# A streaming encoder layer on one core: stick-breaking products partly on GpSimd, the causal mask as a TensorE matmul, and another spread of the filler work

## The chip, the cores and the metric

One core of a Trainium2 chip runs the whole program. The metric is device time in microseconds, from one launch. The engines are called by the names of the profile: PE (TensorE matmuls), PEld (its weight loads), DVE (VectorE), ACT (ScalarE), POOL (GpSimd) and SP, whose queue issues the DMAs.

## The reference

One layer for 1024 prompt tokens and 64 sample tokens (the sample also sees 1024 cached keys), all in f32. Two groups of heads work side by side: four heads of differential attention and eight of stick-breaking attention.

```
h = rmsnorm(x) * (1 + scale1) + shift1;  u = h @ w_in         # q, k, v of both groups
z = (q . k) / 8                                               # stick-breaking heads
log_keep = where(k_pos < q_pos, log_sigmoid(-z), 0)
between  = reverse_cumsum(log_keep) - log_keep                # over the keys behind this one
w        = where(k_pos < q_pos, exp(log_sigmoid(z) + between), 0)
osb      = w @ v
x = x + gate1 * rmsnorm(concat(od, osb) @ w_out)
x = x + gate2 * rmsnorm(relu(h2 @ w_up)^2 @ w_down)
```

In words: the weight of a key is sigmoid(z) of its own, times the product of sigmoid(-z) over all keys between it and the query. Keys at or behind the query's own place count as nothing: their sigmoid(z) must be 0 and their sigmoid(-z) must be 1.

## The kernel before

**Exactness.** f32 operands are cut into a rounded part and a rest (`split`, L62 to L65: ACT makes the rounded copy `hi`, DVE, or GpSimd where `el` says so, subtracts it to get `lo`), and a product is two or three matmuls that add up in PSUM.

**Stages.** First come the modulation vectors and the first projections, then eight units of attention, u = 0 to 3 for the differential heads and u = 4 to 7 for the stick-breaking heads (two heads each), then the output projection (`py`) and the feed-forward network (`pu`, `pd`) for 870 us.

**A unit** is a list of steps. For u of 4 and more a step is `Stick(u, q, hd)`: query blocks t = 2q and 2q + 1 (128 rows each) of head hd. For each t and each chunk of up to 512 keys, `qk` (L571) makes the scores `pz` with two matmuls, ACT takes `s` = sigmoid(z) and `k` = sigmoid(-z) (L738, L739). Then `earlier` (L717) puts 0 into `s` and 1 into `k` on and above the diagonal of the last 128 columns, with two selects on GpSimd. Then `stick` (L705) goes over the chunks from the last one (c = n - 1) to the first: DVE runs a product scan over `k` from right to left (L712), carries it on from the chunk behind, and multiplies `s` by the scanned `k` (L713); one column between two chunks is done on GpSimd (L715). There are 12 chunks for each unit and head, 96 in all, with 1 chunk for t up to 3 and 2 chunks above. Later `apply` (L745) transposes `s` by PE (`pt`, L586), splits the result into `ah` and `al`, multiplies by the values (`po`, L759 and L760) and writes the output columns `mx` (L778, L779).

`Sample(u)`, one in each unit, does the 64 sample tokens against the cache, with scores `pzS`, and for u of 4 and more calls `stick` as well, with three chunks of 512, 512 and 64.

**Order.** Steps overlap: `apply` of one step is merged with `score` of the next (L1013). Each yields its cost, and `Filler.spend` emits that much of other work in between: the projections of the units to come (`proj`, matmuls at L303 to L305, three groups g for each unit) and 12 pieces of modulation rows (`rows`, matmuls at L201 that wait for 1 MB of weights by DMA). The ratio of filler to step cost is set so that the next marked projection is done in time (L1010), from the steps' `cost`. The filler list puts 2, 2, 2, 2, 1 and 3 pieces of `rows` behind the last projection of units 2 to 7 (L994). A scheduler then sets each engine's order.

**V.** `proj_v` (L519) transposes the projected values by PE into a PSUM bank (`pnv`), copies them to `ov` for the output, and splits the bank into the two halves of `V`, the rest on DVE (L542, by L65).

**Buffers.** Tiles `s` and `k` come from one tag "s" with 11 buffers of 128 x 512; the scores use two PSUM banks of the tag "qk". All GpSimd work stands in one queue: selects, the column products, the query pads `qz` (L442), the rests of weight splits (128 x 1024, `wq`, `wk`, `wv`, `wo`) and of the cached values `cv`.

## Time and profile before

| | |
|---|---|
| Time, median of 3 runs | 1587.48 us (1587.13 to 1589.22) |
| Profiled execution, its own time | 1589.58 us |
| Its span, first to last instruction | 1587.9 us |
| PE busy | 1517.0 us (96%), 8682 matmuls |
| DVE busy | 987.2 us (62%) |
| ACT busy | 703.3 us (44%) |
| POOL busy | 366.7 us (23%) |
| Mean granted TensorE clock | 0.973 of 2.4 GHz |

Busy time of an engine is the time in which one of its instructions was open, a wait inside the instruction included. Matmuls overlap each other, so a duration of a PE row is longer than the distance to the next one.

### The profile page before, as it was taken

The page shows a single profiled execution, that of the slowest core. Times are in us where ns is not written, and L with a number is a line of the kernel's source. Part 1 is how long each engine was busy: PE and PEld are TensorE (multiplying, and loading weights), DVE is VectorE, ACT ScalarE, POOL GpSimd, SP SyncE. Part 2 cuts the span into 40 slices and gives each one's busy share as a digit, 9 for nine tenths or more (in the row PEclk, how much of TensorE's full clock was granted, in tenths as well). Part 3 has the DMA queues.
Part 4 walks back from the last instruction along what each step waited for, and adds up shares of the span by engine and source line. Part 5 has one row for each costly group of instructions (what it writes and reads, how often), then busy time and mean ns, then how long its engine had stood idle before and what let it go on. Part 6 is the DMA issues. An engine that isn't in the chain of part 4 may idle for free.

```text
span 1587.9 us, 23684 instructions
## 1 busy us (share of the span) xinstructions
PE 1517.0 (96%) x8682; PEld 1357.9 (86%) x8682; DVE 987.2 (62%) x1880; ACT 703.3 (44%) x1665; POOL 366.7 (23%) x580
## 2 busy tenths in 40 slices
PE   6899999999999999789999999999999999999998
PEld 3689988988888889667889888999999899999896
DVE  3777676778789888995552455445544445544447
ACT  3867675766666667656563221121221121221132
POOL 0444352526353434451120000000000000000003
PEclk9999999998999999879999999999999999999999
DMA  9322142432322222364220222021111011111025
GB/s 309 115 60 87 55 116 84 135 95 76 95 74 85 69 70 78 103 208 161 97 63 27 80 80 78 17 79 53 54 42 52 28 41 53 54 41 53 27 80 179
DMA packets 152518, 133.22 MB, mean 84 GB/s; under 512 B 11233, under 2 KB 136274, under 8 KB 152402
## 3 DMA queue, kind: packets, MB, share of 16 engines
q1 hardware_dynamic: 152402, 131.71, 27.2%
q8 instruction: 68, 1.11, 0.3%
q14 instruction: 48, 0.39, 0.1%
HBM read 108.59 MB, written 23.09 MB: 83 GB/s over the span
## 4 chain that ended last, share of the span: by engine, by line
PE 74%; DVE 12%; issue 4%; ACT 3%; DMA 2%; POOL 1%; SPq 0%; POOLq 0%; DVEq 0%; ACTq 0%
PE pu L303 8%; PE pu L304 8%; PE pu L305 8%; PE pd L1145 8%; PE pd L1146 8%; PE pd L1148 7%; DVE k L712 4%; PE py L1059 2%; PE py L1060 2%; PE pt L586 2%; DVE s L713 2%; PE py L1062 2%; PE pq L304 1%; PE pq L303 1%; PE pq L305 1%
## 5 line engine op out<-in xcount | busy, mean ns | idle before, releaser
L1152 DVE TENSOR_TENSOR acc<-pd,acc 128x512 f32<-128x512 f32 x252 | 171.9, 687 | 113.3 <-PE pd L1148 107.2
L1130 ACT ACTIVATE sq<-pu 128x384 f32<-128x384 f32 (+1 forms) x96 | 45.2, 471 | 310.8 <-PE pu L305 310.8
L1131 DVE TENSOR_TENSOR sq<-sq 128x384 f32<-128x384 f32 (+1 forms) x96 | 72.1, 751 | 174.7 <-ACT sq L1130 174.7
L65 DVE TENSOR_TENSOR al<-pt,ah 128x512 fp32r<-128x512 f32 (+2 forms) x128 | 75.5, 599 | 25.7 <-ACT ah L64 24.9
L575 PE MATMUL pz<-K,Q 128*128 128x512 f32 (+2 forms) x192 | 74.8, 393 | 6.4 <-ACT k L739 2.2
L64 ACT CAST ah<-pt 128x512 fp32r<-128x512 f32 (+2 forms) x128 | 65.4, 523 | 33.6 <-PE pt L586 23.2
L586 PE MATMUL pt<-ident,s 128*128 128x128 f32 x432 | 73.7, 288 | 3.3 <-DVE s L713 2.6
L624 ACT ACTIVATE s<-s,mn 128x512 f32<-128x512 f32 (+3 forms) x96 | 58.5, 611 | 26.7 <-DVE mn L660 25.4
L576 PE MATMUL pz<-Kl,qz 128*128 128x512 f32 (+2 forms) x192 | 69.8, 369 | 0.0
L712 DVE TENSOR_TENSOR_SCAN k<-k 128x127 f32<-128x127 f32 (+3 forms) x64 | 62.1, 980 | 4.3 <-POOL k L720 4.0
L713 DVE TENSOR_TENSOR s<-s,k 128x383 f32<-128x383 f32 (+3 forms) x96 | 62.9, 662 | 1.4
L586 PEld LDWEIGHTS pt<-ident,s 128*128 128x128 f32 x432 | 53.1, 147 | 7.6 <-DVE s L713 3.3
L65 DVE TENSOR_TENSOR rl<-sq,rh 128x384 fp32r<-128x384 f32 x64 | 35.7, 558 | 37.9 <-ACT rh L64 37.9
L738 ACT ACTIVATE s<-pz 128x512 f32<-128x512 f32 (+2 forms) x96 | 48.1, 501 | 16.5 <-PE pz L576 12.0
L575 PEld LDWEIGHTS pz<-K,Q 128*128 128x128 f32 x192 | 38.3, 200 | 15.1 <-ACT k L739 4.5
L64 ACT CAST rh<-sq 128x384 fp32r<-128x384 f32 x64 | 32.9, 514 | 40.2 <-DVE sq L1131 38.2
L739 ACT ACTIVATE k<-pz 128x512 f32<-128x512 f32 (+2 forms) x96 | 48.4, 504 | 4.9 <-DVE k L712 4.0
L442 POOL CAST qz<-Q 64x256 fp32r<-64x256 f32 x64 | 34.7, 542 | 66.3 <-PE pz L576 63.9
L760 PE MATMUL po<-al,V 128*128 128x256 f32 (+1 forms) x160 | 43.5, 306 | 6.7 <-DVE al L65 6.6
L759 PE MATMUL po<-ah,V 128*128 128x256 f32 (+1 forms) x160 | 44.9, 292 | 0.5 <-ACT ah L64 0.5
L720 POOL TENSOR_SCALAR_AFFINE_SELECT s<-s 128x128 f32<-128x128 f32 x64 | 30.1, 470 | 63.6 <-ACT s L738 62.9
L660 DVE CUSTOM_DVE_ANT_0 s<-pz,T 128x512 f32<-128x512 f32 (+3 forms) x64 | 37.2, 585 | 10.8 <-PE pz L576 10.3
(1227 smaller groups left out, 5211.3 us busy)
## 6 DMA issues: line engine op xcount, KB each, us to landing
arr<-in_w_ada SPq DMA_DIRECT2D x16, 512.0 KB
arm<-in_w_ada SPq DMA_DIRECT2D x16, 512.0 KB
ar<-in_w_ada SPq DMA_DIRECT2D x10, 512.0 KB
mixD<-mx SPq DMA_DIRECT2D x32, 128.0 KB
xr<-in_x_prompt SPq DMA_DIRECT2D x16, 256.0 KB
xD<-xr SPq DMA_DIRECT2D x16, 256.0 KB
xy<-xD SPq DMA_DIRECT2D x8, 512.0 KB
out_y_prompt<-xy SPq DMA_DIRECT2D x16, 256.0 KB
```

What stands on the lines that cost most here:

```text
L64: (eh or nc.scalar.copy)(hi, src)
L65: (el or nc.vector).tensor_tensor(lo, src, fr(hi), ALU.subtract)
L303: mm(ps[:, :n], lhsT=wh[:, k, :], rhs=hh[:, k, :n], start=(k == 0), stop=False)
L304: mm(ps[:, :n], lhsT=wh[:, k, :], rhs=hl[:, k, :n], start=False, stop=False)
L305: mm(ps[:, :n], lhsT=wl[:, k, :], rhs=hh[:, k, :n], start=False, stop=(k == 7))
L575: mm(ps[:, :w], lhsT=S["Q"][m][:, qt], rhs=S["Kd"][m][:, c0 : c0 + w], start=True, stop=False)
L586: nc.tensor.transpose(pt[:kr, i * P : (i + 1) * P], a, ident)
L712: nc.vector.tensor_tensor_scan(k, k, k, 1.0 if c == n - 1 else kp[c + 1][:, 0:1], ALU.mult, ALU.bypass)
L1145: mm(ps, lhsT=rh[:, off : off + P], rhs=wh[:, cols], start=(j == 0), stop=False)
L1146: mm(ps, lhsT=rh[:, off : off + P], rhs=wl[:, cols], start=False, stop=(m == 8 and end))
L1148: mm(ps, lhsT=rl[:, off : off + P], rhs=wh[:, cols], start=False, stop=end)
L1152: nc.vector.tensor_tensor(acc[m][:, cols], ps, acc[m][:, cols], ALU.add)
```

## The change

Five things are changed. (1) 72 of the 108 products `s * k` go from DVE to GpSimd: for the prompt all but chunk 0 of the odd t (32 stay on DVE), for the sample two of three. (2) The selects of the prompt's steps go away. `qk` gets a third matmul for the last chunk of each t, with the identity in bf16 as stationary operand and a tile `later` that is -1e30 on and above the diagonal: it adds -1e30 to the scores that must not count, so that the sigmoids themselves are 0 and 1. The sample keeps its selects. (3) The split of `V` reads the copy `ov` in SBUF and not the PSUM bank, and its rest is made on GpSimd. (4) The two halves of a stick step's output are added in `mx` itself, where ACT puts one half first; a tile `ot` goes away. (5) The sample's steps are given smaller costs (2.5 for 6.3, and 0.26 or 0.4 of the yields inside), and the 12 pieces of `rows` stand one behind each of g = 1 and g = 2 of units 2 to 7.

```diff
+    identb, later = (sb.tile([P, P], BF16, name=n) for n in ("identb", "later"))
+    nc.vector.tensor_copy(identb, ident)
+    nc.vector.memset(later, 0.0)
+    nc.gpsimd.affine_select(later, later, pattern=[[-1, P]], compare_op=ALU.is_gt, fill=-BIG, base=0, channel_multiplier=1)
...
     def proj_v(u, g, wv):
...
-        src = ptv[:, : ms.stop - ms.start]
+        src = o[:, : ms.stop - ms.start]
...
-        split(src, h_, l_)
+        split(src, h_, l_, el=nc.gpsimd)
...
-    def qk(u, m, t, c0, w, name):
+    def qk(u, m, t, c0, w, name, mask=False):
...
-        mm(ps[:, :w], lhsT=QZ[m][:, (t % 2) * P : (t % 2 + 1) * P], rhs=S["Kl"][:, c0 : c0 + w], start=False, stop=True)
+        mm(ps[:, :w], lhsT=QZ[m][:, (t % 2) * P : (t % 2 + 1) * P], rhs=S["Kl"][:, c0 : c0 + w], start=False, stop=not mask)
+        if mask:
+            mm(ps[:, w - P : w], lhsT=identb, rhs=later, start=False, stop=True)
...
-    def stick(s, kp):
+    def stick(s, kp, last):
...
             nc.vector.tensor_tensor_scan(k, k, k, 1.0 if c == n - 1 else kp[c + 1][:, 0:1], ALU.mult, ALU.bypass)
-            nc.vector.tensor_tensor(s[c][:, : w - 1], s[c][:, : w - 1], kp[c][:, 1:w], ALU.mult)
+            eng = nc.vector if last and c == 0 else nc.gpsimd
+            eng.tensor_tensor(s[c][:, : w - 1], s[c][:, : w - 1], kp[c][:, 1:w], ALU.mult)
...
-                    ps = qk(u, hd, t, c0, w, f"pz{self.name}{t}{c}")
+                    ps = qk(u, hd, t, c0, w, f"pz{self.name}{t}{c}", c == len(ch) - 1)
...
-                earlier(s[-1][:, -P:], kp[-1][:, -P:], P)
-                stick(s, kp)
+                stick(s, kp, t % 2 == 1)
...
-            ot = brief([P, 256], f"ot{self.name}", "so2", bufs=1)
-            nc.scalar.copy(ot[r], po[o, 0:256])
-            nc.vector.tensor_tensor(mx[r], po[r, 0:256], ot[r], ALU.add)
+            nc.scalar.copy(mx[r], po[o, 0:256])
+            nc.vector.tensor_tensor(mx[r], po[r, 0:256], mx[r], ALU.add)
...
-            self.u, self.name, self.cost = u, f"S{u}", 6.3
+            self.u, self.name, self.cost = u, f"S{u}", 2.5
...
-            yield from self.cache()
+            for c in self.cache():
+                yield 0.4 * c
...
-    others = {2: (rows, 2, 2), 3: (rows, 2, 2), 4: (rows, 2, 2), 5: (rows, 2, 2), 6: (rows, 1, 1), 7: (rows, 3, 3)}
     for u in range(8):
         for g in range(3):
             if u + g:
                 fill.add(proj(u, g), 12, (u, g))
-            if g == (2) and u in others:
-                gen, n, c = others[u]
-                fill.add(some(gen, n), c, "end" if u == 7 else None)
+            if u > 1 and g > 0:
+                fill.add(some(rows, 1), 1, "end" if u == 7 else None)
```

The scheduler's order moves with it. **GpSimd's queue** in unit 6, last pair of query blocks (q = 3), head 1, t = 6 and 7; `s_316_1` is the tile `s` of q = 3, hd = 1, t = 6, chunk 1. Before:

```order
L720 AFFINE_SELECT s_316_1_7909<-s_316_1_7909 128x128 [waits Activation_49]
L720 AFFINE_SELECT k_316_1_7911<-k_316_1_7911 128x128 [waits Activation_49]
L715 TENSOR_TENSOR s_316_0_7908<-s_316_0_7908,k_316_1_7911 128x1 [waits DVE_49]
L442 CAST qz_494<-Q_7605 64x256 [waits PE_49,Pool_49]
L720 AFFINE_SELECT s_317_1_7965<-s_317_1_7965 128x128 [waits Activation_49,Pool_49]
L720 AFFINE_SELECT k_317_1_7967<-k_317_1_7967 128x128 [waits DVE_49,Activation_49]
```

Now:

```order
L722 TENSOR_TENSOR s_316_1_7767<-s_316_1_7767,k_316_1_7769 128x383 [waits DVE_49,Pool_49]
L724 TENSOR_TENSOR s_316_0_7766<-s_316_0_7766,k_316_1_7769 128x1
L722 TENSOR_TENSOR s_316_0_7766<-s_316_0_7766,k_316_0_7768 128x511 [waits DVE_49]
L448 CAST qz_501<-Q_7543 64x256 [waits PE_49,Pool_49]
L722 TENSOR_TENSOR s_317_1_7812<-s_317_1_7812,k_317_1_7814 128x511 [waits DVE_49,Pool_49]
L724 TENSOR_TENSOR s_317_0_7811<-s_317_0_7811,k_317_1_7814 128x1
L65 TENSOR_TENSOR V_7740<-ov_7847,V_7740 128x3x128 [waits Activation_49]
```

The selects, which waited for ACT and stood ahead of the scans, are gone; products that wait for DVE's scans stand there, and the rest of `V`.

**DVE's queue** for the same two query blocks (a scan is listed as SCALAR_TENSOR_TENSOR). Before:

```order
L712 SCALAR_TENSOR_TENSOR k_316_1_7911<-k_316_1_7911 128x384 [waits Pool_49]
L713 TENSOR_TENSOR s_316_1_7909<-s_316_1_7909,k_316_1_7911 128x383 [waits DVE_49]
L712 SCALAR_TENSOR_TENSOR k_316_0_7910<-k_316_0_7910,k_316_1_7911 128x511
L488 SCALAR_TENSOR_TENSOR Q_7604<-pq_7973,Q_7604 64x384 [waits Activation_49]
L713 TENSOR_TENSOR s_316_0_7908<-s_316_0_7908,k_316_0_7910 128x511 [waits DVE_49]
L65 TENSOR_TENSOR al_300_7905<-pt_300_7899,ah_300_7904 128x512 [waits Activation_49]
L779 TENSOR_TENSOR mx_20_7759<-po_21_7764,ot_21_7893 64x256 [waits Activation_49]
L464 COPY ov_7946<-pnv_7942 128x384 [waits DMAHW1_49,PE_49]
L488 SCALAR_TENSOR_TENSOR Q_7605<-pq_7973,Q_7605 64x384 [waits Activation_49]
L65 TENSOR_TENSOR al_301_7929<-pt_301_7923,ah_301_7928 128x512 [waits Activation_49]
L712 SCALAR_TENSOR_TENSOR k_317_1_7967<-k_317_1_7967 128x512 [waits Pool_49]
```

Now:

```order
L720 SCALAR_TENSOR_TENSOR k_316_1_7769<-k_316_1_7769 128x384 [waits Activation_49]
L720 SCALAR_TENSOR_TENSOR k_316_0_7768<-k_316_0_7768,k_316_1_7769 128x511 [waits DVE_49,Pool_49]
L65 TENSOR_TENSOR al_300_7763<-pt_300_7757,ah_300_7762 128x512 [waits Activation_49]
L65 TENSOR_TENSOR al_301_7787<-pt_301_7781,ah_301_7786 128x512 [waits Activation_49]
L720 SCALAR_TENSOR_TENSOR k_317_1_7814<-k_317_1_7814 128x512 [waits Activation_49,Pool_49]
L720 SCALAR_TENSOR_TENSOR k_317_0_7813<-k_317_0_7813,k_317_1_7814 128x511 [waits DVE_49,Pool_49]
L722 TENSOR_TENSOR s_317_0_7811<-s_317_0_7811,k_317_0_7813 128x511 [waits DVE_49]
```

The scan of chunk 0 now follows the scan of chunk 1 directly, at the moment in which GpSimd has the product of chunk 1 to do; a scan no longer waits for a select, and one product in four chunks is left on DVE.

**PE's queue** in unit 7, the last unit, where query pair q = 1 is scored. Now:

```order
L311 MATMUL pq_8197<-h1h_126,wq7l 128x320
L581 MATMUL pz_1020_8233<-K_7641,Q_7542 128x384 [waits Activation_49]
L582 MATMUL pz_1020_8233<-Kl_7643,qz_500 128x384
L584 LDWEIGHTS identb
L584 MATMUL pz_1020_8233<-later,identb 128x128
L309 MATMUL pq_8197<-h1h_126,wq7h 128x320
```

The mask's matmul stands behind the two of the scores, and matmuls of the last projections stand around them. Behind the first `po` matmul of unit 7 there were 24 projection matmuls before, of 1656; now there are 72.

## Rows read from the trace of the kernel before

**Rows 1.** Busy time in stretches (us, then each engine's busy time, granted clock, DMA).
```profile
370.00:460.00 90.00, 85.50 (x563) 79.06 (x562) 73.67 (x128) 58.56 (x144) 41.38 (x71) 0.94 0.26 78
460.00:550.00 90.00, 81.04 (x546) 75.81 (x545) 82.79 (x130) 55.31 (x133) 39.32 (x66) 0.96 0.28 80
550.00:640.00 90.00, 84.76 (x557) 79.64 (x557) 80.49 (x133) 62.51 (x149) 37.17 (x67) 0.94 0.29 80
640.00:720.00 80.00, 67.01 (x349) 53.80 (x347) 74.90 (x117) 49.08 (x106) 37.61 (x40) 0.82 0.49 158
...
370.00:720.00 350.00, 318.30 (x2010) 288.31 (x2008) 311.86 (x505) 225.46 (x529) 155.47 (x243) 0.92 0.32 97
```

**Rows 2.** Chain of waits, shares by line, from 370 to 720 and from 100 to 370.
```profile
by line: DVE k L712 17.5%; DVE s L713 7.8%; issue 7.3%; DVE al L65 5.3%; PE pt L586 3.4%; PE po L760 2.3%; DVE ml L65 2.3%; PE pq L303 2.2%; PE pq L304 2.1%; PE pq L305 2.1%; PE pz L575 2.0%; DVE sk L712 2.0%; PE pz L576 1.8%; PE pv L305 1.
...
by line: PE po L602 6.8%; DMA arr<-in_w_ada 5.8%; PE pt L586 5.4%; PE pq L303 5.2%; PE pq L304 5.1%; PE pv L303 5.1%; PE pk L304 5.1%; PE pk L303 5.1%; PE pv L305 5.0%; PE pq L305 5.0%; PE pk L305 4.9%; PE pv L304 4.9%; PE pz L576 4.4%; PE 
```

**Rows 3.** Stretches of 20 us, one with PE full and one without, columns as in rows 1.
```profile
590.00:610.00 20.00, 20.00 (x133) 19.60 (x133) 19.31 (x30) 13.50 (x35) 6.89 (x17) 1.00 0.11 31
...
670.00:690.00 20.00, 14.24 (x70) 11.29 (x71) 18.45 (x21) 11.49 (x21) 13.75 (x15) 0.65 0.41 143
```

**Rows 4.** DVE's groups from 370 to 720: count, busy us, mean ns, idle before.
```profile
L713 DVE TENSOR_TENSOR s<-s,k 128x511 f32<-128x511 f32 x48 | 41.9, 874 | 0.7
...
L713 DVE TENSOR_TENSOR s<-s,k 128x383 f32<-128x383 f32 x16 | 9.1, 569 | 0.2
...
L713 DVE TENSOR_TENSOR s<-s,k 128x255 f32<-128x255 f32 x16 | 6.8, 428 | 0.2
...
L713 DVE TENSOR_TENSOR s<-s,k 128x127 f32<-128x127 f32 x16 | 5.7, 356 | 0.2
L713 DVE TENSOR_TENSOR ss<-ss,sk 128x511 f32<-128x511 f32 x8 | 5.5, 691 | 0.0
...
L65 DVE TENSOR_TENSOR V<-pnv,V 128x384 fp32r<-128x384 f32 x7 | 3.8, 542 | 0.0
```

**Rows 5.** The products' line on DVE, whole program: ns least/median/most.
```profile
L713 DVE TENSOR_TENSOR s<-s,k x96: 260/664/2802, 370.6 to 703.8; 128x511 f32<-128x511 f32 x48, 128x127 f32<-128x127 f32 x16, 128x255 f32<-128x255 f32 x16, 128x383 f32<-128x383 f32 x16
...
L713 DVE TENSOR_TENSOR sst<-sst,skt x4: 225/225/2197, 457.2 to 674.4; 128x63 f32<-128x63 f32 x4
```

**Rows 6.** The selects' line on POOL, ns least/median/most, whole program.
```profile
L720 POOL TENSOR_SCALAR_AFFINE_SELECT s<-s x64: 282/295/1976, 369.4 to 687.0; 128x128 f32<-128x128 f32 x64
L720 POOL TENSOR_SCALAR_AFFINE_SELECT k<-k x64: 282/292/1243, 369.6 to 688.1; 128x128 f32<-128x128 f32 x64
```

**Rows 7.** What DVE's scans (L712) waited for, us and times, whole program.
```profile
  POOL k L720: 4.0, 9
```

**Rows 8.** POOL's elementwise rests: `cv` (least/median/most) and one weight (mean).
```profile
L65 POOL TENSOR_TENSOR cv<-cvr,cv x16: 1276/1291/2192, 137.5 to 666.3; 128x512 fp32r<-128x512 f32 x16
...
L65 POOL TENSOR_TENSOR wk5l<-wk5r,wk5h 128x1024 fp32r<-128x1024 f32 x1 | 2.3, 2347 | 0.1
```

**Rows 9.** In order of time, DVE and then POOL, 674 to 683: start, us, instruction.
```profile
674.39 2.20 DVE L713 TENSOR_TENSOR sst<-sst,skt 128x63 f32<-128x63 f32 x1
...
680.68 3.06 DVE L712 TENSOR_TENSOR_SCAN k<-k 128x384 f32<-128x384 f32 x1
...
674.11 2.40 POOL L65 TENSOR_TENSOR wo0l<-wo0r,wo0h 128x1024 fp32r<-128x1024 f32 x1
...
679.61 3.31 POOL L65 TENSOR_TENSOR wo1l<-wo1r,wo1h 128x1024 fp32r<-128x1024 f32 x1 [0.65 <-ACT wo1h L64]
```

**Rows 10.** PE in order of time: score matmuls of 128 columns, projection matmuls of 320.
```profile
601.13 0.28 PE L576 MATMUL pz<-Kl,qz 128*128 128x128 f32 x1
601.25 0.39 PE L304 MATMUL pk<-h1l,wk7h 128*128 128x384 f32 x1
...
455.45 0.31 PE L303 MATMUL pq<-h1h,wq5h 128*128 128x320 f32 x1
455.60 0.31 PE L304 MATMUL pq<-h1l,wq5h 128*128 128x320 f32 x1
```

More of the change, by code (lines that the diff above doesn't have):

```diff
@@ L856, in score @@
                         scale=1.0, scalar=(3e38 if c == 0 else mn[:, c - 1 : c]), accum_out=mn[:, c : c + 1])
-                    yield 0.65
+                    yield 0.26
                 l = brief([P, 3], f"sl{u}", "sl", bufs=2)
@@ L868, in score @@
                     nc.scalar.activation(kp[c], ps, AF.Sigmoid, scale=-1.0)
-                    yield 0.65
+                    yield 0.26
                 for hd in range(2):
@@ L872, in score @@
                     earlier(s[2][r], kp[2][r], TS)
-                stick(s, kp)
+                stick(s, kp, True)
             self.s = s
@@ L879, in apply @@
             parts = [([s[c][:, i * P : (i + 1) * P] for i in range(4)], P, f"{self.name}{c}", None) for c in range(2)]
-            yield from apply_rows(po, parts + [([s[2]], TS, f"{self.name}2", None)], self.V)
-            o2 = brief([P, 256], f"so2{u}", "so2", bufs=1)
+            for c in apply_rows(po, parts + [([s[2]], TS, f"{self.name}2", None)], self.V):
+                yield 0.4 * c
+            o2 = small([P, 384], f"so2{u}", "kf")[:, :256]
             od = brief([P, P], f"sod{u}", "od", bufs=1)
```

## The prediction, made before the changed kernel was run

> **What bounds the kernel now.** I read first the busy time in stretches, to see where PE is not full. From 720 us on PE is, at the full clock, and nothing there is touched. The change works on the stick-breaking units, 370 to 720 us [rows 1]: of 350 us PE is busy for 318.3, so 31.7 are idle, and its mean clock is 0.92, so up to 28 us more are lost in matmuls at the lower level of 1.2 GHz. DVE is busy for 311.9 of 350. The last of the four units is the worst: PE 67.0 of 80 us at a clock of 0.82, DVE 74.9.
>
> Next the chain of waits in that stage [rows 2]: the scans have 17.5%, the products `s` 7.8%, `al` 5.3%, all on DVE; no line of PE has over 3.4%. So DVE sets the pace, but not everywhere. From 590 to 610 PE is busy for 20.0 of 20 us at clock 1.00, and a DVE that is freed gives nothing there; from 670 to 690 it is at 14.2 and 0.65, with DVE at 18.5 and POOL at 13.8 [rows 3]. The fully busy stretches are some 130 us of the stage, the others some 220.
>
> Then DVE and POOL side by side in order of time, for what the two do to each other [rows 9]. A product of 63 elements, 0.225 us at its median [rows 5], takes 2.20 us while POOL's `wo0l` runs from 674.11 to 676.51, and ends with it. A scan takes 3.06 us beside `wo1l`, which itself takes 3.31 where its like takes 2.35 [rows 8]. So a POOL instruction and a DVE instruction that reads two SBUF operands do not run beside each other. Products and scans both are of that kind; `al`, which reads PSUM, is not.
>
> **The change part by part.**
>
> *Products leave DVE.* By width, 24 of the 48 of 511, all 16 of 383, 8 of the 16 of 255 and all 16 of 127 go [rows 4]: 24 x 0.874 + 9.1 + 8 x 0.428 + 5.7 = 39.2 us of busy time out of 63.5, or 62%. The products have 7.8% of a chain of 350 us, 27.3 us; 62% of that is **17 us** off the path. The upper end is that all 39 us come off, the lower end nothing. Four `ss` products (2.8 us) are inside these bounds.
>
> *Products come to POOL.* No row before shows one there. The nearest is `cv`, also two f32 operands of 512 columns: 1.29 us; 1024 columns take 2.35 [rows 8]. The line through both gives 1.02 us for 383, 0.76 for 255 and 0.49 for 127 columns: 24 x 1.29 + 16 x 1.02 + 8 x 0.76 + 16 x 0.49 = 61 us, and 7 for the sample. The rests of `V` in the stage, 7 of 384 and 4 of 256 columns, add 10: 78 us in all. Away go 128 selects of 0.29 [rows 6], 38 us. POOL works for 40 us more, and POOL's work stands in DVE's way. How much of the 40 us stretches DVE has two ends: nothing, if POOL waits each time, and all 40. The nearest row is the 511 product itself: 0.874 on average against a median of 0.664 for the line [rows 4, 5], a quarter of its time spent in stretching. I take a quarter, 10 us, and of that the 220/350 that lie where DVE sets the pace: **+6 us**.
>
> *Selects go.* Scans waited 4.0 us for them, 9 times [rows 7]; they stood in POOL's queue behind weight rests of 2.35 us. Half of it is on the path: **-2 us**. Next late is the scan's other wait, for ACT's `k`.
>
> *The mask on PE.* 64 matmuls of 128 columns, each with a weight load of its own. No bf16 one is in the trace; two f32 score matmuls of 128 columns are 0.12 us apart [rows 10], so 64 x 0.12 = 7.7 us at most, and 0 where PE waits anyway. PE is full for 130 of 350 us: **+3 us**.
>
> *`V` and `mx`.* The rests of `V`, 0.54 us each [rows 4], leave DVE; nothing waits for them, so I give 0. Their cover is that a unit's values are used a unit later. What is new: the next copy into the single buffer `ov` now waits for POOL, and DVE's queue stands behind that copy. In `mx` ACT takes over DVE's wait for the store of the last `mx`; 0.
>
> *Filler.* Behind the first `po` of unit 7 stand 72 projection matmuls instead of 24. One of 320 columns is 0.15 us from the next [rows 10]: 48 x 0.15 = 7 us of PE work go from units in which PE is often full to the one in which it is idle for 13 of 80 us [rows 1]. I take **-5 us**, between 0 and -7. The pieces of modulation rows come one by one instead of in pairs. In the stretch 100 to 370 us the weight transfers for them, `arr`, have 5.8% of the chain [rows 2], 270 x 0.058 = 15.7 us. Between -15 and +5, a piece that comes at a worse moment, I take **-3 us**: each piece still waits for 1 MB, only not two in a row.
>
> *Setup.* The two bf16 tiles are a handful of instructions beside the first transfers: 0.
>
> Sum: -17 + 6 - 2 + 3 - 5 - 3 = -18 us. Against the profiled execution's own 1589.6 (span 1587.9) that is 1571.6; that execution lies 2.1 us over the median of the runs, 1587.5. The forecast for the median is 1587.5 - 18 = 1569.5, said as **1570 us**.
>
> **The rivals.**
>
> *The two engines stand in each other's way (slower).* The order now puts a scan of DVE right behind the scan that releases POOL's product, for each pair of chunks; both want to start at once. Each time POOL comes first, the scan waits up to 1.29 us, and where a weight rest of 2.35 us stands ahead of a product, transposes wait for the product. If 0.9 of the 40 added us come on the path, with no gain by filler, it is -17 - 2 + 3 + 36 = +20, 1607 us. Without filler's gain the sign turns when 16 of the 40 us come on the path. For it: rows 9. Against it: the stretching so far is a quarter, and POOL was open for 155 of 350 us with much of it waiting.
>
> *Nothing comes of it (no change).* Count the time in which either engine holds the other off. POOL gets 40 us more; the moved products were 39 us on DVE, so the sum stays. If that sum and not DVE alone sets the length of the stage, the -17 is given back by the holds, and -2 + 3 - 3 = -2 is left: some 1586 us. For it: in the worst unit both are at work nearly all the time (74.9 and 37.6 of 80). Against it: the sum is below the stage's length as soon as the waits are not counted in it twice. The Trainium skill, SBUF — State Buffer, section "SBUF: two separate sides", states this as a rule: DVE, when it reads two SBUF inputs, and GpSimd share a pair of ports under an exclusive lock that is held for the whole instruction. The trace agrees in the two cases of rows 9 (2.20 and 3.06 us); that rule would make it 1586.
>
> *DVE stops being the bound (much faster).* All 39 us come off the path, PE gets its 32 idle us and its clock back for the greater part: -39 + 6 - 2 + 3 - 5 - 3 = -40, 1548 us. The floor is near: 31.7 idle and 28 of clock, less 8 for the mask, 52 us. For it: DVE's 17.5% for scans hang on the same queue. Against it: 130 us of the stage are PE-full already.
>
> That the change does not do what it says is out: in the new order the selects are gone from POOL's queue and the products stand there.
>
> **How the numbers follow.** Forecast (1560 to 1580): 0.50. Much faster (1540 to 1560): 0.21. Nothing (1582 to 1592): 0.13. Slower: 0.16. A change of this kernel under 0.2%, 3.2 us, cannot be told from none. Faster by more takes the first two cases, 0.71; the third is "same", 0.13; the last "slower", 0.16. The range leaves out some 0.2: the lower end 1549 is the much faster case's own value, the upper end 1594 takes in the case of nothing and the start of the slower one (+6).
>
> **What the new profile would show.** DVE's busy time from 370 to the end of the stage falls by 40 to 50 us, and the stage from 350 to about 335. POOL's rises above 155, with 511-wide products of 1.3 us, some of 2 to 3 where a scan stands beside them. Some scans get longer, by up to the 1.3 us of a product. PE's clock in the last unit rises above 0.82. Wrong would be: the scans' mean going up by as much as the products took (then the no-change or slower rival), ACT waiting for POOL to free `s` and `k` (a cause that I have priced at nothing), or the gain lying in the stretch before 370 us.

## The result, and the profile after

| | kernel before | changed kernel |
|---|---|---|
| Time, median of 4 runs each | 1588.16 us (1587.13 to 1589.22) | 1605.04 us (1601.72 to 1612.79) |
| Ratio | | 1.0113, 95% interval 1.0074 to 1.0153 |
| Profiled execution, its own time | 1589.58 us | 1601.72 us |
| Its span | 1587.9 us | 1600.0 us |
| Mean granted TensorE clock | 0.973 | 0.977 |

The change makes the kernel 18 us slower by the ratio and 16.9 us by the medians, where 18 us faster was forecast; the time lies outside the range. The profiled execution is the fastest of the four, 12 us above the one of the kernel before. Two lines of the new page, the span and the busy times:

```profile
span 1600.0 us, 23676 instructions
PE 1524.8 (95%) x8746; PEld 1353.0 (85%) x8746; DVE 964.5 (60%) x1786; ACT 706.3 (44%) x1667; POOL 413.4 (26%) x549
```

DVE fell from 987.2 to 964.5 us and POOL rose from 366.7 to 413.4, as the moved products should do; PE is busy for 7.8 us longer, with 64 matmuls more.

**Where the time went.** Three instructions mark the same points of the program in each profile: the last score of a differential sample (`sst`, its last start), the first matmul of the output projection (`py`, first start) and the first of the feed-forward network (`pu`, first start). Rows by tile: count, least/median/most ns, first and last start in us. The kernel before:

```profile
L854 DVE CUSTOM_DVE_ANT_0 sst<-pzS,Tst,smn x4: 284/284/285, 146.7 to 365.5; 128x64 f32<-128x64 f32 x4
...
L1059 PE MATMUL py<-wo0h,mh x18: 394/398/629, 694.2 to 803.7; 128*128 128x512 f32 x18
...
L303 PE MATMUL pu<-h2h,wu00h x24: 306/336/426, 807.5 to 839.5; 128*128 128x384 f32 x16, 128*128 128x320 f32 x8
```

The changed kernel:

```profile
L862 DVE CUSTOM_DVE_ANT_0 sst<-pzS,Tst,smn x4: 276/280/284, 154.2 to 378.5; 128x64 f32<-128x64 f32 x4
...
L1066 PE MATMUL py<-wo0h,mh x18: 389/397/628, 707.8 to 815.9; 128*128 128x512 f32 x18
...
L309 PE MATMUL pu<-h2h,wu00h x24: 306/335/425, 819.6 to 851.7; 128*128 128x384 f32 x16, 128*128 128x320 f32 x8
```

The last differential sample stands at 378.5 us instead of 365.5, the output projection at 707.8 instead of 694.2, the feed-forward network at 819.6 instead of 807.5, and from there to the end it is 780.4 us in both. So in this pair of profiles 13 us are lost before the stick-breaking units, and the stage that the change works on takes 329.3 us against 328.7. (How far one execution moves such a mark by itself is told with the next four runs.) From 100 to 365.5 us PE gets through less work in the same time at the same clock (columns as in rows 1, before and then after):

```profile
100.00:365.50 265.50, 257.81 (x1684) 238.23 (x1683) 187.03 (x540) 174.48 (x516) 104.44 (x168) 0.97 0.34 98
```

```profile
100.00:365.50 265.50, 252.34 (x1621) 230.47 (x1622) 184.78 (x521) 171.07 (x505) 108.79 (x174) 0.97 0.32 94
```

It does 1621 matmuls instead of 1684. In the stick-breaking stage, in stretches that begin 13 us later than those of [rows 1]:

```profile
383.00:473.00 90.00, 86.38 (x585) 77.48 (x584) 71.63 (x112) 61.75 (x150) 48.97 (x58) 0.98 0.29 85
473.00:563.00 90.00, 83.36 (x561) 74.70 (x560) 72.23 (x109) 57.52 (x134) 48.30 (x49) 0.98 0.26 77
563.00:653.00 90.00, 85.78 (x581) 78.13 (x580) 72.74 (x108) 56.33 (x136) 44.66 (x51) 0.96 0.29 85
653.00:733.00 80.00, 62.63 (x341) 49.38 (x341) 72.15 (x105) 52.95 (x117) 51.24 (x42) 0.87 0.47 145
383.00:733.00 350.00, 318.15 (x2061) 279.69 (x2060) 288.75 (x431) 228.55 (x534) 193.16 (x198) 0.95 0.32 97
```

DVE is at 288.8 us of 350 instead of 311.9, POOL at 193.2 instead of 155.5 and the clock at 0.95 instead of 0.92, yet PE is busy for 318.2 us as before (318.3). The groups that answer to [rows 4, 8], from 370 to 720 us, with the scans of 511 columns of the kernel before ahead of them:

```profile
L712 DVE TENSOR_TENSOR_SCAN k<-k,k 128x511 f32<-128x511 f32 x32 | 42.3, 1322 | 0.0
...
L720 DVE TENSOR_TENSOR_SCAN k<-k,k 128x511 f32<-128x511 f32 x32 | 52.5, 1640 | 1.7
...
L722 POOL TENSOR_TENSOR s<-s,k 128x511 f32<-128x511 f32 x24 | 31.4, 1309 | 5.5 <-DVE k L720 4.5
...
L722 POOL TENSOR_TENSOR s<-s,k 128x383 f32<-128x383 f32 x16 | 17.5, 1091 | 44.0 <-DVE k L720 40.4 <-PE pt L594 2.6 <-DVE Bm L234 1.0
...
L724 POOL TENSOR_TENSOR s<-s,k 128x1 f32<-128x1 f32 x32 | 24.2, 755 | 0.0
```

The product of 511 elements takes 1.31 us on POOL (forecast 1.29). The scans of 511 went from a mean of 1322 ns to 1640. ACT waited for POOL's products for 1.0 us before its second sigmoid (L748), in two waits. The shares of the chain by line, which answer to [rows 2]:

```profile
by line: DVE k L720 9.3%; PE pt L594 6.6%; PE po L768 4.3%; PE pv L309 3.7%; PE po L767 3.6%; PE pv L310 3.4%; PE pv L311 3.4%; PE pq L309 3.4%; PE pq L311 3.2%; PE pq L310 3.2%; DMA mixD<-mx 3.1%; PE pz L581 3.1%; DVE sk L720 3.0%; DMA mst
```

The scans fell from 17.5% to 9.3%, the products' line is gone from the head of the list, and the places behind are PE's.

### The profile page after: what moved, and what is told of

Same layout as the page of the kernel before. It is cut to its first block, busy times and chain, and to the rows that moved or that the text cites. A ratio compares the mean times of both kernels' runs of the same rounds, so it can differ in the third digit from the quotient of the medians.

```text
span 1600.0 us, 23676 instructions
## 1 busy us (share of the span) xinstructions
PE 1524.8 (95%) x8746; PEld 1353.0 (85%) x8746; DVE 964.5 (60%) x1786; ACT 706.3 (44%) x1667; POOL 413.4 (26%) x549
## 4 chain that ended last, share of the span: by engine, by line
PE 68%; DVE 6%; ACT 2%; issue 2%; DMA 1%; POOL 1%; DVEq 0%; POOLq 0%; ACTq 0%
PE pu L309 8%; PE pu L310 8%; PE pu L311 8%; PE pd L1152 8%; PE pd L1153 8%; PE pd L1155 7%; DVE k L720 2%; PE py L1067 2%; PE py L1066 2%; PE py L1069 2%; PE pt L594 2%; PE pv L309 1%; PE po L768 1%; PE pv L311 1%; PE pv L310 1%
## 5 line engine op out<-in xcount | busy, mean ns | idle before, releaser
L722 POOL TENSOR_TENSOR s<-s,k 128x511 f32<-128x511 f32 (+3 forms) x64 | 63.5, 994 | 80.3 <-DVE k L720 73.5
L747 ACT ACTIVATE s<-pz 128x512 f32<-128x512 f32 (+2 forms) x96 | 48.0, 500 | 17.6 <-PE pz L584 6.3
L720 DVE TENSOR_TENSOR_SCAN k<-k,k 128x511 f32<-128x511 f32 x32 | 52.5, 1640 | 1.7
L748 ACT ACTIVATE k<-pz 128x512 f32<-128x512 f32 (+2 forms) x96 | 47.9, 499 | 4.0 <-DVE sk L720 1.8
L768 PEld LDWEIGHTS po<-al,V 128*128 128x128 f32 x160 | 31.4, 196 | 15.9 <-DVE al L65 13.3
```

What stands on the lines that cost most here:

```text
L720: nc.vector.tensor_tensor_scan(k, k, k, 1.0 if c == n - 1 else kp[c + 1][:, 0:1], ALU.mult, ALU.bypass)
```

## The experiments

After the first reading there were three theories: the new sample costs and filler list lose the time before 370 us; the products on GpSimd lose it by holding DVE's scans; the rest of `V` on GpSimd delays the differential units. Ratios are to the kernel before in the same comparison, on the same chip.

| run | what it has of the change | median, us | before, us | ratio, 95% interval |
|---|---|---|---|---|
| fill_only | part 5 (costs, rows) | 1601.57 | 1585.89 | 1.0109 (1.0094 to 1.0124) |
| no_fill | all but part 5 | 1587.81 | 1585.89 | 1.0015 (1.0005 to 1.0025) |
| mask_prod | mask, products, mx | 1585.91 | 1585.89 | 1.0005 (0.9989 to 1.0021) |
| mask_mx | mask, mx | 1589.16 | 1585.89 | 1.0015 (0.9997 to 1.0034) |
| rows_only | rows one by one | 1586.71 | 1585.72 | 1.0006 (0.9993 to 1.0018) |
| cost_only | sample costs | 1600.64 | 1585.72 | 1.0087 (1.0063 to 1.0112) |
| no_rows | all but the rows | 1599.48 | 1585.72 | 1.0082 (1.0063 to 1.0102) |
| no_cost | all but the sample costs | 1593.42 | 1585.72 | 1.0045 (1.0029 to 1.0061) |
| cost_diff | costs x 0.4, units 0 to 3 | 1601.41 | 1585.84 | 1.0092 (1.0072 to 1.0113) |
| cost_stick | costs x 0.4, units 4 to 7 | 1583.51 | 1585.84 | 0.9976 (0.9959 to 0.9994) |
| cost_x15 | costs x 1.5, all units | 1593.72 | 1585.84 | 1.0049 (1.0026 to 1.0072) |
| cost_u0 | costs x 0.4, unit 0 | 1596.33 | 1585.70 | 1.0069 (1.0050 to 1.0088) |
| cost_u123 | costs x 0.4, units 1 to 3 | 1601.48 | 1585.70 | 1.0102 (1.0083 to 1.0121) |
| cost_x095 | costs x 0.95, all units | 1590.70 | 1586.64 | 1.0027 (1.0013 to 1.0041) |
| change_stickcost | all, but costs of units 0 to 3 as before | 1598.92 | 1585.70 | 1.0081 (1.0063 to 1.0099) |
| prod_not7 | mask_prod, unit 7's products on DVE | 1584.29 | 1585.84 | 0.9989 (0.9971 to 1.0008) |
| prod_all | mask_prod, all 108 products on POOL | 1589.64 | 1586.64 | 1.0022 (1.0000 to 1.0043) |
| mask_prod_stickcost | mask_prod and cost_stick | 1589.82 | 1585.70 | 1.0025 (1.0010 to 1.0040) |

### Four parts of the change

fill_only is the kernel before with these lines alone:

```diff
-            self.u, self.name, self.cost = u, f"S{u}", 6.3
+            self.u, self.name, self.cost = u, f"S{u}", 2.5
-            yield from self.cache()
+            for c in self.cache():
+                yield 0.4 * c
-                    yield 0.65
+                    yield 0.26
...
-            if g == (2) and u in others:
-                gen, n, c = others[u]
-                fill.add(some(gen, n), c, "end" if u == 7 else None)
+            if u > 1 and g > 0:
+                fill.add(some(rows, 1), 1, "end" if u == 7 else None)
```

> Kernel before with part 5 alone (smaller sample costs, rows one by one). Theory 1, the filler: the changed kernel stands 13 us later than the kernel before already when the stick-breaking stage begins (last differential sample 365.5 to 378.5 us), so the loss comes from part 5: 1598 to 1601 us, with the first stick scan near 380 us. Theory 2, the products: the scans' mean rose from 1322 to 1640 ns where GpSimd has the products, the loss is there, and part 5 gives what was forecast for it: 1580 to 1586 us. Theory 3, the rest of V on GpSimd delays the differential units: 1580 to 1588 us here.

no_fill has all the rest, mask_prod leaves `V` out as well, mask_mx the products too:

```diff
-            eng = nc.vector if last and c == 0 else nc.gpsimd
-            eng.tensor_tensor(s[c][:, : w - 1], s[c][:, : w - 1], kp[c][:, 1:w], ALU.mult)
+            nc.vector.tensor_tensor(s[c][:, : w - 1], s[c][:, : w - 1], kp[c][:, 1:w], ALU.mult)
```

> The changed kernel without part 5 (filler list and sample costs as before): mask, products, V and mx. Theory 1, the filler: the stage 100 to 370 us is again as before, so the loss of 13 us is gone, 1585 to 1592 us. Theory 2, the products: 1603 to 1610 us. Theory 3, V on GpSimd: the first stick scan stays near 380 us, 1600 to 1605 us.

> Mask on TensorE, products shared with GpSimd, mx in place; V and filler as before. Theory 1, the filler: the stick-breaking stage alone gains about nothing or little, 1582 to 1590 us. Theory 2, the products: 1600 to 1610 us. Theory 3, V on GpSimd: as theory 1 here, 1582 to 1590 us; the difference to the kernel that has V too (the run without part 5) is then 10 us or more.

> Mask on TensorE and mx in place alone; all products stay on DVE. Theory 1 and theory 3: the selects go, scans no longer wait for GpSimd (4.0 us before), 64 small matmuls come: 1583 to 1588 us. Theory 2, the products: also 1583 to 1588 us here, and 15 us or more under the run with the products on GpSimd.

Part 5 alone costs 15.7 us, and without it the rest of the change is 2 us from the kernel before. Theory 1 holds, theory 3 falls, and so does theory 2 as a cause of the loss (mask_mx is 1 us over what all three gave it, fill_only half a us over theory 1). 2 us for the rest and 15.7 for part 5 make 17.6, near the whole, 16.9 by the medians and 18 by the ratio. The three marks of fill_only:

```profile
L855 DVE CUSTOM_DVE_ANT_0 sst<-pzS,Tst,smn x4: 283/284/285, 153.9 to 375.0; 128x64 f32<-128x64 f32 x4
...
L1059 PE MATMUL py<-wo0h,mh x18: 392/398/628, 708.2 to 816.5; 128*128 128x512 f32 x18
...
L303 PE MATMUL pu<-h2h,wu00h x24: 306/335/425, 820.2 to 852.3; 128*128 128x384 f32 x16, 128*128 128x320 f32 x8
```

It stands 9.5 us later at the last differential sample (375.0 against 365.5) and 14.0 at `py`.

How far such a mark can be trusted is seen in two of these runs. mask_mx and mask_prod give PE the same matmuls in the same order up to 387 us, and their marks stand at 370.1 and 361.0 us: up to there the granted clock was 0.95 in the one execution and 0.99 in the other. So a mark is only compared at a like clock. The changed kernel's 378.5 is 8 us behind mask_mx, both at 0.95; fill_only's 375.0 is 9.5 us behind the kernel before, both at 0.97. no_fill, which has the rest of `V` on GpSimd, stands at 365.4 (0.98).

### Which piece of part 5

rows_only has the last piece of the diff of fill_only, cost_only the pieces ahead of it; no_rows and no_cost are the changed kernel without the one and without the other.

> Kernel before with the new filler list alone (one piece of modulation rows behind each of g = 1 and 2 of units 2 to 7), sample costs as before. Part 5 alone cost 15.7 us (1601.57 against 1585.89 in the same runs). Theory 1a, the rows: each piece waits for 1 MB of weights wherever it stands, and 12 places instead of 6 break into 12 stretches of projections: 1595 to 1602 us. Theory 1b, the sample's costs: with 6.3 and 0.65 a sample, whose cache work leaves TensorE gaps, got filler; with 2.5 and 0.26 it gets 0.4 of that, the gaps stay open: about the kernel before here, 1583 to 1589 us.

> Kernel before with the smaller sample costs alone (2.5 for 6.3, yields of 0.26 and 0.4), the rows as before. Theory 1a, the rows: 1583 to 1589 us here. Theory 1b, the sample's costs: 1597 to 1603 us.

> The changed kernel with the filler list of before; the sample costs stay small. Theory 1a, the rows: 1585 to 1591 us, as the changed kernel without all of part 5. Theory 1b, the sample's costs: 1600 to 1606 us.

> The changed kernel with the sample costs of before; rows one by one. Theory 1a, the rows: 1598 to 1606 us. Theory 1b, the sample's costs: 1585 to 1591 us.

The rows alone cost 1 us, with an interval that takes in none, the sample's costs alone 15: theory 1b. But the two are not independent. no_cost lies in neither theory's range, between them, and no_rows half a us under 1b's. In the whole change the rows matter by about 5 us: 1593.42 without the costs against 1587.81 without both, 5.6 from two comparisons, or 4.8 by the ratios.

Where the loss stands is not the same in each kernel. The mark of no_rows:

```profile
L862 DVE CUSTOM_DVE_ANT_0 sst<-pzS,Tst,smn x4: 265/280/285, 154.9 to 363.1; 128x64 f32<-128x64 f32 x4
```

At 363.1 us nothing is lost yet, and `py` begins at 701.1 instead of 694.2, `pu` at 817.4 instead of 807.5: with the same small costs and the rows as before, this profile has its loss behind the differential units.

### Which samples, and whether it is the amount

The costs and yields of a sample are scaled by a factor `f`, in cost_diff only for units 0 to 3, in cost_stick only for 4 to 7, in cost_x15 for all:

```diff
+            self.f = 0.4 if u < 4 else 1.0
+            self.cost = 6.3 * self.f
...
+            for c in self.cache():
+                yield self.f * c
```

> Kernel before with the sample's costs at 0.4 in units 0 to 3 alone. Theory A1, the loss arises in the differential units, where the changed kernel had its 13 us (first stick scan 370.0 to 380.3): 1595 to 1602 us. Theory A2, it arises in the stick-breaking units, where a sample scans three chunks for each head pair: 1584 to 1590 us.

> Kernel before with the sample's costs at 0.4 in units 4 to 7 alone. Theory A1, the loss arises in the differential units: 1584 to 1590 us. Theory A2, in the stick-breaking units: 1593 to 1602 us.

> Kernel before with the sample's costs and yields times 1.5 (9.45 for 6.3), so the other way than the change. The costs at 0.4 cost 14.9 us alone (1600.64 against 1585.72). Theory A, the sample's steps are long for TensorE and want the filler that their cost buys: more cost gives as much or more, 1575 to 1587 us. Theory B, the planner's order was simply best at the old costs, and any other value moves it off: 1592 to 1605 us.

On the kernel before, the loss comes from the samples of units 0 to 3 (A1); in units 4 to 7 the smaller costs gain 2.3 us (interval 1 to 6.5; half a us under A1's range). Dearer samples lose 7.9 us, so theory A, more filler for a sample is as good or better, falls. The marks of cost_diff:

```profile
L856 DVE CUSTOM_DVE_ANT_0 sst<-pzS,Tst,smn x4: 276/284/285, 152.4 to 370.1; 128x64 f32<-128x64 f32 x4
...
L1062 PE MATMUL py<-wo0h,mh x18: 389/398/497, 703.3 to 814.2; 128*128 128x512 f32 x18
...
L303 PE MATMUL pu<-h2h,wu00h x24: 306/335/425, 818.0 to 850.0; 128*128 128x384 f32 x16, 128*128 128x320 f32 x8
```

It is 4.6 us later at the last differential sample, little against the scatter of that mark, 9.1 at `py` and 10.5 at `pu`. So the greater part of this loss shows behind that point, though the last step with another cost is the one that makes the mark, while the changed kernel was late there already.

The next runs set the factor for sample 0, for samples 1 to 3, and for all samples at 0.95; change_stickcost is the changed kernel with `f` at 1.0 for units 0 to 3:

```diff
-            self.f = 0.4 if u < 4 else 1.0
+            self.f = 0.4 if u == 0 else 1.0
```

> Kernel before with the cost of sample 0 alone at 0.4 (its steps stand in unit 1). Theory 1, the first sample: the differential run is 7 us behind already when sample 0's scores come (147.5 against 140.7 us): 1593 to 1602 us. Theory 2, units 2 and 3: 1584 to 1588 us.

> Kernel before with the costs of samples 1 to 3 at 0.4. Theory 1, the first sample: 1584 to 1589 us. Theory 2, units 2 and 3: 1593 to 1602 us.

> The whole change with one thing put back: the samples of units 0 to 3 have the costs of before. Theory A, the loss of the change is the differential samples' costs: 1584 to 1593 us, 12 to 20 us under the changed kernel. Theory B, the parts are entangled and the change is slow for another reason too: above 1597 us.

> Kernel before with the sample's costs and yields times 0.95 (5.99 for 6.3). Theory A, the amount of filler around a sample counts: a twelfth of the step to 0.4, which cost 15 us, so 1586 to 1588 us. Theory B, the same work in another order is what costs, and the order of before was a good one: 1590 us or more.

Neither theory stands: cost_u0 lies in the range of theory 1, cost_u123 in that of theory 2. Sample 0 alone costs 10.6 us and samples 1 to 3 alone 15.8, which do not add up to the 15.6 of both. Putting back the costs of units 0 to 3 in the whole change, with small ones for units 4 to 7, gains at most about 5 us (1.0081 for 1.0113, overlapping intervals, theory B); putting back all of them gained about 11 (1.0045). So in the whole change, other than on the kernel before, the samples of units 0 to 3 do not account for the loss. And a change of the costs by a twentieth, for which the amount of filler would have given 1 us, costs 4.1 us (theory B). That speaks for the other order as what costs, and not for less filler around a sample: with the factor 0.95 some 1,050 of PE's 8,450 matmuls stand at another place than before, with cost_diff some 2,500, counted in the two orders with the numbers of the tiles left out. An amount that happened to be best at its old value would lose in both directions too; against it stand cost_stick, where less is faster, and the two losses that do not add. No run held the amount and changed the order alone. Of the seven settings of these costs that were tried on the kernel before, six are slower by 4 to 16 us and one is faster by 2.

### What the products gain

The chain of mask_mx, from 370 to 720 us:

```profile
by line: DVE k L720 11.0%; issue 6.2%; PE pt L594 5.9%; DVE s L721 4.1%; PE po L767 3.6%; DVE al L65 3.1%; PE pq L309 3.0%; DVE sk L720 3.0%; PE po L766 3.0%; PE pq L310 2.9%; PE pq L311 2.9%; PE pk L309 2.7%; PE pz L581 2.7%; PE pk L310 2.
```

With the mask alone, and all products on DVE, the scans' share is at 11.0% instead of 17.5, the products' at 4.1 instead of 7.8, and the time is the same or 3 us longer. The share that left the chain was not time that came off. Now the marks, mask_mx and then mask_prod (the 9 us between them at the first mark go with the clock, as said above):

```profile
L860 DVE CUSTOM_DVE_ANT_0 sst<-pzS,Tst,smn x4: 283/284/284, 149.8 to 370.1; 128x64 f32<-128x64 f32 x4
...
L1065 PE MATMUL py<-wo0h,mh x18: 393/398/628, 697.8 to 804.2; 128*128 128x512 f32 x18
...
L309 PE MATMUL pu<-h2h,wu00h x24: 306/335/425, 808.0 to 840.0; 128*128 128x384 f32 x16, 128*128 128x320 f32 x8
```

```profile
L861 DVE CUSTOM_DVE_ANT_0 sst<-pzS,Tst,smn x4: 283/284/284, 146.0 to 361.0; 128x64 f32<-128x64 f32 x4
...
L1066 PE MATMUL py<-wo0h,mh x18: 394/398/628, 685.1 to 799.4; 128*128 128x512 f32 x18
...
L309 PE MATMUL pu<-h2h,wu00h x24: 306/335/425, 803.1 to 835.2; 128*128 128x384 f32 x16, 128*128 128x320 f32 x8
```

From the last differential sample to `py` it is 327.7 us without the moved products and 324.1 with them, from `py` to `pu` 110.2 and 118.0: what the stage may gain is given back behind it. Each profile is one execution, and runs scatter by some us, so the medians decide: 1589.16 and 1585.91, with overlapping intervals. Scans and products in mask_mx, mask_prod and prod_all, over the whole program:

```profile
L720 DVE TENSOR_TENSOR_SCAN k<-k 128x127 f32<-128x127 f32 (+3 forms) x64 | 63.1, 987 | 7.3 <-ACT k L747 6.9
...
L720 DVE TENSOR_TENSOR_SCAN k<-k,k 128x511 f32<-128x511 f32 x32 | 43.4, 1357 | 0.0
...
L721 DVE TENSOR_TENSOR s<-s,k 128x127 f32<-128x127 f32 (+3 forms) x96 | 54.3, 571 | 1.7
```

```profile
L720 DVE TENSOR_TENSOR_SCAN k<-k 128x127 f32<-128x127 f32 (+3 forms) x64 | 64.9, 1016 | 8.9 <-ACT k L748 8.2
...
L720 DVE TENSOR_TENSOR_SCAN k<-k,k 128x511 f32<-128x511 f32 x32 | 49.2, 1536 | 1.1
...
L722 DVE TENSOR_TENSOR s<-s,k 128x511 f32<-128x511 f32 (+1 forms) x32 | 24.6, 768 | 0.6
...
L722 POOL TENSOR_TENSOR s<-s,k 128x511 f32<-128x511 f32 (+3 forms) x64 | 60.4, 945 | 94.4 <-DVE k L720 79.2 <-issue 5.9 <-PE po L768 4.3
```

```profile
L720 DVE TENSOR_TENSOR_SCAN k<-k 128x127 f32<-128x127 f32 (+3 forms) x64 | 71.3, 1123 | 18.0 <-ACT k L748 17.5
...
L720 DVE TENSOR_TENSOR_SCAN k<-k,k 128x511 f32<-128x511 f32 x32 | 50.1, 1566 | 0.8
...
L722 POOL TENSOR_TENSOR s<-s,k 128x127 f32<-128x127 f32 (+3 forms) x96 | 100.9, 1055 | 72.6 <-DVE k L720 62.5 <-PE pt L594 4.9 <-DVE Bm L234 2.6
```

29.7 us of products leave DVE (54.3 to 24.6) and the scans get 7.6 longer (63.1 + 43.4 to 64.9 + 49.2): a quarter is given back by the engines holding each other. DVE's busy time as a whole falls by 12.3 us only, from 983.8 to 971.5 on the two pages; other instructions, `ml`, `Am` and `mh`, are 8.8 us longer in that execution. prod_all moves the next step:

```diff
-            eng = nc.vector if last and c == 0 else nc.gpsimd
+            eng = nc.gpsimd
```

> Mask, products and mx as in the run with these alone, but all 108 products on GpSimd. DVE loses another 27 us of products (24 x 0.885 + 8 x 0.419 and two of ss), GpSimd gets 24 x 1.21 + 8 x 1.0 = 37 us. Theory A, DVE's free time is worth something and the two engines hold each other for a quarter of it: 1578 to 1584 us. Theory B, nothing comes of it, because TensorE's work and the end of the stage set the time: 1584 to 1589 us. Theory C, the engines stand in each other's way or transposes wait for GpSimd: above 1590 us.

24.6 us more leave DVE, scans get 7.3 us longer, and the time is 1589.64 us, at the border between theories B and C and outside A: freeing DVE further shows no gain. How a hold looks, in mask_prod, in order of time on DVE and then on POOL (start, us, instruction):

```profile
583.38 1.99 DVE L720 TENSOR_TENSOR_SCAN k<-k,k 128x511 f32<-128x511 f32 x1
...
588.88 2.21 DVE L720 TENSOR_TENSOR_SCAN k<-k,k 128x511 f32<-128x511 f32 x1
...
593.51 1.28 DVE L720 TENSOR_TENSOR_SCAN k<-k,k 128x511 f32<-128x511 f32 x1
...
583.43 0.86 POOL L722 TENSOR_TENSOR s<-s,k 128x383 f32<-128x383 f32 x1 [3.76 <-DVE k L720]
...
584.25 1.10 POOL L724 TENSOR_TENSOR s<-s,k 128x1 f32<-128x1 f32 x1
...
588.93 1.09 POOL L722 TENSOR_TENSOR s<-s,k 128x511 f32<-128x511 f32 x1 [2.06 <-DVE k L720]
...
593.62 1.83 POOL L722 TENSOR_TENSOR s<-s,k 128x383 f32<-128x383 f32 x1 [2.54 <-DVE k L720]
```

The scans at 583.38 and 588.88 take 1.99 and 2.21 us, 0.7 and 0.9 more than the one at 593.51 (1.28), while POOL's product, which starts 0.05 us after them, takes its 0.86 and 1.09. At 593.62 it is the other way round: the scan takes 1.28 and the product of 383 elements 1.83. And the product of a single column at 584.25 takes 1.10 us, to the end of the scan beside it.

What stands behind the stage in mask_prod: the rounding of the output weights `wo1`, its rest on POOL, the sending of `wo5`, and the longest piece of the chain from 685 to 715 us:

```profile
L64 ACT CAST wo1h<-wo1r x1: 1074/1074/1074, 670.2 to 670.2; 128x1024 fp32r<-128x1024 f32 x1
...
L65 POOL TENSOR_TENSOR wo1l<-wo1r,wo1h x1: 2347/2347/2347, 675.6 to 675.6; 128x1024 fp32r<-128x1024 f32 x1
...
L300 SPq DMA_DIRECT2D wo5r<-in_w_out x1: 422/422/422, 692.1 to 692.1; - x1
...
694.07 7.75 DMA wo6r<-in_w_out
```

`wo1h` is there at 671.3 us, but POOL begins its rest at 675.6, behind products; `wo4`, which waits for that rest, is sent at 678.0, when it ends. `wo5` is sent at 692.1 us, as late as before (692.2), although `py` begins 9 us earlier, and the chain then has 7.75 us for the transfer of `wo6`. `wo5` itself waits for nothing: eight sends of `mst`, the pieces of the mix, stand ahead of it in SP's queue from 682.58 to 692.08, the first held until 682.5 by a product on DVE and the next ones mainly by DVE's rests `ml`. To test POOL's part in this, in prod_not7 the products of unit 7 went back to DVE:

```diff
-            eng = nc.vector if last and c == 0 else nc.gpsimd
+            eng = nc.vector if u == 7 or last and c == 0 else nc.gpsimd
```

> Mask, products and mx as in the run with these alone (1585.91 us), but all products of unit 7 on DVE again. In that run the output projection begins at 685.1 us instead of 694.2, and then TensorE waits: wo1l starts on GpSimd 4.3 us after wo1h is there, behind products, the raw buffers come free late, wo5r is sent at 692.1 us, and its first 25 us of matmuls stand still for 10 us instead of 4. Theory A, the gain of the products is given back there, because GpSimd's products of the last unit stand ahead of the rests of the output weights: 1578 to 1584 us, with wo5 sent before 688 us. Theory B, the products gain nothing because scans stretch as much as the products took: 1584 to 1589 us.

```profile
L300 SPq DMA_DIRECT2D wo5r<-in_w_out x1: 367/367/367, 686.2 to 686.2; - x1
```

`wo5` comes 6 us earlier, and `py` to `pu` is at 111.5 us again (689.5 to 801.0), 6.5 less, while the stage ahead is 2.6 us longer (326.7). The time is 1584.29 us, on the border of the two ranges, and cannot be told from mask_prod or from the kernel before. `wo4`, which hangs on POOL's queue, is sent 1.4 us earlier (676.6); between it and `wo5` three `mst` sends stand now. That POOL's queue holds `wo4` is shown; that it makes `wo5` late, or costs time, is not.

> Mask, products, mx in place, and the small costs for the samples of units 4 to 7 alone; V, the filler list and the other samples as before. If the gain of these costs alone (1583.51 against 1585.84) adds to mask and products (1585.91 against 1585.89): 1580 to 1585 us. If the end of the stage is set by the output weights (wo5 sent at 692 us), nothing is added: 1584 to 1588 us.

1589.82 us: above both ranges. The gain of cost_stick does not add to the products, one more case of two edits whose effects do not add. What beats both kernels is cost_stick by itself, 1583.51 us, 2.3 us under the kernel before (0.9976).

## Why the prediction was wrong

**The step that failed is "Filler".** The sum gave part 5 -5 us for the projections that reach unit 7 and -3 for the rows, and the sample's costs no price of their own. Part 5 alone measured +15.7 us. The costs changed the order of PE's work from 84 us on (fill_only), and the working looked at its end alone, the 72 projection matmuls behind the first `po` of unit 7. They got there; the stage is not shorter for it (329.3 against 328.7 us). The rows one by one are +1 us on the kernel before, inside the bounds of -15 and +5; inside the whole change about +5, at their edge. Of the signs that the prediction named, "the gain lying in the stretch before 370 us" came true with a loss in place of a gain. No rival had it: the one on the slower side gave 1607 us, near the 1605 that came, but by holds between DVE and POOL, and the runs without part 5 show that those did not do it.

**Products, holds.** The holds came out near their size. 10 us of stretching were taken, a quarter of the 40 us that POOL was to work more; the scans got 7.6 us longer for 29.7 us of products that left DVE, and POOL's busy time in the stage rose by 37.7 in the changed kernel. That the quarter fits is in part luck: it set the mean of the 511-wide products, 0.874, against 0.664, the median of products of all four widths. The 511-wide ones have a median of 0.692 in the same trace, which makes it a fifth. The 6 us that were put on the path are shown by no run by themselves. The -17 us was wrong: 7.8% of a chain was taken as time that comes off. With the mask alone the same line was down to 4.1% with no gain, and with products and mask together the time was 1.0005 of that before. So the net of -11 for both terms is 0 to -3 (mask_prod less mask_mx, 3.3 us, overlapping). The rival "nothing comes of it" said 1586, and mask_prod has 1585.91, but not by its mechanism: the holds took a quarter and not all. What the Trainium skill states in SBUF — State Buffer, section "SBUF: two separate sides", that the loser is blocked for the other's whole instruction, agrees with the rows at 583.38, 588.88 and 593.62 nearly: the loser is longer by 0.71, 0.93 and 0.97 us (1.83 against 0.86) beside instructions of 0.86, 1.09 and 1.28. The prediction drew 1586 us from that rule, the whole gain given back; what the scans gave back was a quarter of it.

**Mask and selects.** +3 and -2 were forecast, mask_mx, which has `mx` too, measured +2.4 us by the ratio and 3.3 by the medians (interval from none to 5): within the bounds, and not clear of none.

**`V`, `mx`, setup.** 0 was forecast. no_fill, which has `V`, is 1.9 us above mask_prod, with overlapping intervals: no difference is shown.

**Signs in the stage.** 511-wide products at 1.31 us and POOL at 193 us came as said, as did a clock in the last unit over 0.82 (0.87). ACT's wait for POOL was 1.0 us, rightly put at nothing. DVE fell by 23 us, not 40 to 50, and the stage did not get shorter.

**Open.** Why the new orders are slower is not settled. In the changed kernel PE stands idle for 13.2 us between 100 us and the mark instead of 7.7; five gaps of over 1 us make 9.8 of it, where two made 3.4. Up to 365.5 us the longest of PE's waits are those for the rows' weights, 5.4 us against 3.7, and one of 2.3 us for DVE. The added idle time is 5.5 of the 13 us; in the rest PE is open, 265.3 us for 1710 matmuls against 257.8 for 1684. For no_rows and cost_diff the greater part comes behind that point. That the settings of the costs cost 4 to 16 us is measured, why the old order is a good one is not.

## What to carry to other kernels

In a kernel whose main engine is 96% busy by an order that a planner made, each cost in the planner can be part of the tuned result (here six of seven other settings were slower): price an edit of it by a run, alone, before it travels with other changes, and do not expect two orders' gains to add. An engine's share of the chain of waits says what is last now, not what comes off when it is made shorter: look at which engine's chain is close behind, here PE's own. Work moved to another engine gives back a share in longer instructions where the two engines hold each other (here the scans gave back a quarter; mean against median of one and the same width is a first estimate of it), and can delay whatever else stands in that engine's queue. And a mark in a single profile moves with the granted clock of that execution: compare marks at a like clock.

## What was not expected of the hardware

A product of one column on GpSimd, in the kernel before and in the changed one:

```profile
L715 POOL TENSOR_TENSOR s<-s,k x32: 183/290/2134, 392.5 to 693.4; 128x1 f32<-128x1 f32 x32
...
L724 POOL TENSOR_TENSOR s<-s,k x32: 184/1102/1109, 406.4 to 710.2; 128x1 f32<-128x1 f32 x32
```

Its median went from 290 ns to 1102 ns. All 18 products of over 0.9 us in the changed kernel start beside a scan and end with it: the smallest instruction pays the whole hold. And the time of one and the same kernel followed the granted clock: the kernel before took 1580.63 us in a run at a mean of 0.982 and 1589.16 in one at 0.973, so that two profiles can differ by as much as the parts of this change did.
